# Transposes moved from TensorE to VectorE blocks and DMAs in a one-core hybrid decoder layer

## The chip, the core and the metric

One core of one Trainium2 chip runs the whole layer: TensorE (PE) multiplies matrices, VectorE (DVE) and ScalarE (ACT) work on tiles element by element, GpSimd (POOL) does a few small jobs, and SyncE (SP) issues nearly all of the DMAs. The metric is the device time of one execution in microseconds (us). Lower is better. A time is the median of the runs shown.

## The reference

256 tokens `x` of width 2048 go through one decoder layer in float32: a mixer of mLSTM heads and attention heads, a gated MLP, and a gated addition of a projected side input `p`. Cut to what matters:

```python
h  = rms_norm(x, mix_norm_g)
z  = h @ w_in                                   # 2048 -> 7184 columns
mq, mk, mv, mo, mi, mf, fq, fk, fv, ff = split(z)
ha = mlstm_chunkwise(heads(mq), heads(mk), heads(mv), mi + b, log_sigmoid(mf + b))   # 4 heads of 256
ha = rms_norm(ha, mlstm_out_g) * sigmoid(mo)
qb, kb = rms_norm(fq, fox_q_g), rms_norm(fk, fox_k_g)                                # 8 heads of 128
hb = softmax(qb @ kb.T / sqrt(128) + F[t] - F[s], causal) @ fv    # F: running sum of log_sigmoid(ff + b)
x  = x + concat([ha, hb]) @ w_out                                                   # 2048 -> 2048
a, g = split(rms_norm(x, ffn_norm_g) @ w_up)                                        # 2048 -> 2 x 5632
x  = x + (gelu(causal_dwconv(a)) * g) @ w_down                                      # 5632 -> 2048
x  = x + sigmoid(rms_norm(x, ple_norm_g) @ w_ple_gate) * (p @ w_ple_proj)           # 2048 -> 2048, 256 -> 2048
```

## The kernel before

**Matmuls.** The 256 tokens are two tiles of 128 (NT = 2), the width 2048 is 16 K tiles of 128. Every product is made of three matmuls: weights and activations are each split into a high part `hi` and a remainder `lo`, and hi·hi, hi·lo and lo·hi are summed in PSUM (L291 to L293; L327 to L329 for `quad_group`). The activations stand as the stationary operand, turned (K on the partitions, tokens along the row): `hT`, `catT`, `x2T`, `uT`, `x3T`. So each activation must be transposed between the stage that makes it (tokens on the partitions) and the stage that uses it.

**The stream of weights.** `run_stream` goes through a list of steps. SP loads a block of weights (`raw`, 512 KB, L242), ACT casts it to `hi` (L211), DVE subtracts to get `lo` (L213), PE multiplies. `token_group` makes 8 steps for 512 output columns: a step takes two K tiles and both token tiles, which is 2 x 2 x 3 = 12 matmuls of 128x512. There are 4 raw buffers in the mixing part and 6 in the rest; the split runs 3 (later 4) steps ahead of the matmuls.

**Side work.** Everything else is written as generators in a queue `side`. After each step `pull(2)` advances two of them by one `yield`; a `yield n` puts a generator to sleep for n steps, and `pull(10 ** 6)` runs all to the end. A scheduler then fixes the order of each engine. All DMAs named below are issued by SP in one order, so a load of weights stands behind every small DMA issued ahead of it. Each DMA on SP takes one of eight semaphores in turn and waits for the DMA that had it before.

**Order of the stages.** w_in (attention q, k, v and gates first, then mLSTM q, k, v, o), w_out in four groups of 512 columns (c = 0 to 3), w_up with two passes of w_down, and last the PLE part: for each of four column groups one step of w_ple_proj and eight of w_ple_gate.

**Two ways to transpose stand in the kernel.**

1. On TensorE with an identity matrix (`pe.transpose` into PSUM, then ACT and DVE copy it out): the input (`xT`, L144, in `transpose_x`), the attention weights (`pt`, L657), the gated mLSTM heads (`hap`, L789), `p` (`pTp`, L1118), and column groups 2 and 3 of both residuals (`xT` again, called by `turn_late`), 32 + 24 + 16 + 4 + 32 = 108 transposes of 128x128.
2. On DVE and DMA: `dve.transpose` turns the 32x32 blocks of a tile within their place (L507 for q and k, L843 for the residual), and 16 DMAs of SP carry the blocks to their partitions (`turned`, L870, 32 KB each); L877 (ACT) and L878 (DVE) then scale and split it. The heads' q and k and column groups 0 and 1 of both residuals go this way. `resid(..., nt)` says how many column groups do (`nt` = 2).

Buffers: `mqT0`, `mkT0` and the temporaries `t0` to `t3` have tags of their own; `zb_room` and `sq_rooms` lend the room for the blocks of `turned`.

Of the kernel before, what the change touches and what calls it, by code (L numbers as in the profile page):

```python
# [46 lines left out]
def layer_kernel(  # L47
# [218 lines left out]
    def token_group(w, korder, actT, c0, n, finish, tag="mm", prep=None, load=None, slots=10 ** 6, halved=False):  # L266
# [7 lines left out]
        for bi, (k0, kb) in enumerate(starts):  # L274
            def fn(hi, lo, bi=bi, k0=k0):
                if bi == 0:
                    st["b"] = [(t, 0, n, bank(tag, f"tg{t}")) for t in range(NT)]
                    if halved:
                        st["b"][1:] = [(1, c, c + n // 2, bank(tag, "tg1")) for c in (0, n // 2)]
                final = bi == len(starts) - 1  # L280
                if halved and bi == len(starts) - 2:
                    st["kept"] = [(k0, hi, lo)]
                    return
                for t, c, e, bk in st["b"]:
                    for k, h, l in (st.get("kept", []) if final else []) + [(k0, hi, lo)]:
                        for i in range(h.shape[1]):
                            a = actT()[:, (k + i) % slots, :]
# [3 lines left out]
                            pe.matmul(bk[:, : e - c], ah, h[:, i, c:e], start=first, stop=False)  # L291
                            pe.matmul(bk[:, : e - c], ah, l[:, i, c:e], start=False, stop=False)  # L292
                            pe.matmul(bk[:, : e - c], al, h[:, i, c:e], start=False, stop=last)  # L293
                    if final:
                        finish(t, bk, *((c, e) if halved else ()))
# [74 lines left out]

    dp = ctx.enter_context(tc.tile_pool(name="rows", bufs=1, space=bass.MemoryType.DRAM))
# [10 lines left out]
    with tc.tile_pool(name="mix", bufs=1) as mp:  # L382
        catT = mp.tile([P, KD, 512], F32R, name="catT")
# [99 lines left out]
        def fox_norm(name):  # L483
            def gen():
# [13 lines left out]
                for c in range(2):  # L498
# [3 lines left out]
                    if c == 0:  # L502
                        T = mp.tile([P, 1536], F32, tag="wt", name="fsq")[:, :1024]
                    else:
                        T = mp.tile([P, 4, NT, P], F32, tag="mqT0", name="fsq1").rearrange("p f t r -> p (f t r)")
# [4 lines left out]
                    if name == "fq":  # L510
                        flat = mp.tile([P, 4, NT, P], F32, tag=f"mkT{c}", name="fsy").rearrange("p f t r -> p (f t r)")
                        moved.append((flat, v))
# [17 lines left out]
        g = {}  # L530
# [58 lines left out]
        def row_bcast(tag, h, bufs):  # L589

            v = mp.tile([P, 2, 384], F32, tag=tag, name=tag, bufs=bufs)
            nc.sync.dma_start(out=v.rearrange("p e c -> p (e c)"),
# [3 lines left out]
        def fox_heads():  # L596
            bias, fetched = {}, {}

            def fetch(h0):
                bias[h0] = row_bcast("L", 8 + h0, 3)  # L600
                fetched[h0] = clock[0]

            def first():
                while "em" not in g:
                    yield 1
                for h0 in (0, 2, 4):
# [4 lines left out]
            def gen(pairs):  # L611
                while "em" not in g or len(ready) < 2:
                    yield 1
                zq, zk = zhalves("fq"), zhalves("fk")
# [3 lines left out]
                for h0 in pairs:  # L618
# [35 lines left out]
                    for e in range(2):  # L654
                        pt = bank("aux", "pt")
                        for c in range(3):
                            pe.transpose(pt[:, c * P : (c + 1) * P], L[:, e, c * P : (c + 1) * P], ident)  # L657
                        act.copy(L[:, e], pt[:, 0:384])
                        yield
                    ob = bank("aux", "ob")  # L660
                    for e in range(2):
                        h, o = h0 + e, ob[:, e * 256 : (e + 1) * 256]
                        hs = slice(h * FD, (h + 1) * FD)
                        pe.matmul(o, zv[:, 0, hs], L[:, e, 0:256], start=True, stop=False)  # L664
                        pe.matmul(o[:, 128:256], zv[:, 1, hs], L[:, e, 256:384], start=False, stop=True)
                    for e in range(2):
                        split_T(catT[:, 8 + h0 + e, :], ob[:, e * 256 : (e + 1) * 256])
                    if h0 == 0:
                        fetch(6)
# [7 lines left out]
        def qk_evac(name, grp, done=None):  # L677
            def f(t, b):
                key = name, grp
                if t == 0:  # L680
                    qkT[key] = mp.tile([P, 4, NT, P], F32, name=f"{name}T{grp}")
# [95 lines left out]
        def mlstm_gate(heads):  # L777
            def gen():
                zo, zv = z["mo"], z["mv"]
                for h in heads:  # L780
                    while h not in ha:
                        yield 1
                    bk = bank("aux", "hap")
                    for t in range(NT):
                        hh = zv[:, t, h * 258 : h * 258 + MD]
                        dve.scalar_tensor_tensor(out=hh, in0=hh, scalar=ha[h][:, t : t + 1],
                                                 in1=zo[:, t, h * MD : (h + 1) * MD], op0=ALU.mult, op1=ALU.mult)
                        for i in range(2):
                            pe.transpose(bk[:, i * 256 + t * P : i * 256 + (t + 1) * P],  # L789
                                         hh[:, i * P : (i + 1) * P], ident)  # L790
                    for i in range(2):
                        split_T(catT[:, 2 * h + i, :], bk[:, i * 256 : (i + 1) * 256],
                                scale=g_ml[:, 2 * h + i : 2 * h + i + 1])
# [40 lines left out]
        def resid(c, ssq, dst, gain, room, nt):  # L834
            st = {}

            def f(t, b):
                xc = xs[:, t, c * 512 : (c + 1) * 512]
                dve.tensor_add(xc, b, xc)
                if c < nt:  # L840
                    if t == 0:
                        st["T"], st["Y"] = room()
                    dve.transpose(st["T"][:, :, 4 * t : 4 * t + 4].rearrange("p j f r -> p f j r"),  # L843
                                  xc.rearrange("p (f j r) -> p f j r", f=4, j=4))
# [10 lines left out]
        def turn_late(c, dst, gain):  # L855
            for k0 in (c * 4, c * 4 + 2):
                transpose_x(dst(), k0, gain)
                yield
                yield

        def all_late():
            for job in late:
                yield from job
            late.clear()

        def turned(c, T, Y, dst, gain):

            for n in range(16):
                i, j = divmod(n, 4)
                nc.sync.dma_start(out=Y[32 * j : 32 * j + 32, :, 32 * i : 32 * i + 32], in_=T[32 * i : 32 * i + 32, j])  # L870
                yield
# [15 lines left out]

        kcat = all_k[4:] + all_k[:4]
# [7 lines left out]
        for c in range(4):  # L896
            grp = token_group(w_out, kcat, lambda: catT, c * 512, 512, resid(c, ssq2, get_x2T, g_ffn, zb_room, 2))
            if c == 0:
                grp[4].fn = lambda hi, lo, fn=grp[4].fn: (pull(10 ** 6), fn(hi, lo))
            blocks.extend(grp)  # L900
        run_stream(blocks, 2, ramp=True)
        pull(10 ** 6)
        side.append(all_late())


    with tc.tile_pool(name="ffn", bufs=1) as fp:
# [10 lines left out]
        def tmp(i):  # L917
            return fp.tile([P, 512], F32, tag=f"t{i % 4}", name=f"t{i % 4}")
# [3 lines left out]
        def x2_sums():  # L922
            for i, p in enumerate(S_UP):
                a = tmp(0).rearrange("p (k s) -> p k s", k=2)
                e = tmp(1).rearrange("p (e s) -> p e s", e=4)
# [23 lines left out]
        def up_mid(q):  # L949
            def f(st):  # L950
                t11, t12, t21, t22 = (tmp(i) for i in range(4))
# [23 lines left out]
        def up_evac(q, ag):  # L975
            def f(t, b):
                if ag == 0 and t == 0:
                    sq[q] = fp.tile([P, 2, 4, NT, 4, 32], F32, tag="sq", name="sq")
                z = tmp(2 + t)
# [130 lines left out]
        def load_p():  # L1110
            pr = tmp(3).rearrange("p (t d) -> p t d", t=NT)
            nc.sync.dma_start(out=pr, in_=p[0, 0].rearrange("(t p) d -> p t d", p=P))
            while "bank" not in pT:
                yield 1
            bk = bank("mm", "pTp")
            for k in range(2):
                for t in range(NT):
                    pe.transpose(bk[:, k * 256 + t * P : k * 256 + (t + 1) * P], pr[:, t, k * P : (k + 1) * P], ident)  # L1118
            pT["t"] = x2E.rearrange("p s e c -> p (s e c)")[:, 0:1024].rearrange("p (k c) -> p k c", k=2)
            for k in range(2):  # L1120
                split_T(pT["t"][:, k, :], bk[:, k * 256 : (k + 1) * 256])
            yield

        def down_mid(c, ends):
            def f(st):
                if ends and c == 0:
                    pT["bank"] = True
                xc = [[xs[:, t, (c + n) * 512 : (c + n + 1) * 512] for n in range(2)] for t in range(NT)]
                a, b = tmp(0), tmp(1)
# [11 lines left out]
        def down_end(c, ends):  # L1141
            room = sq_rooms()
            done = [resid(c + n, ssq3, get_x3T, g_ple, lambda n=n: room(n), 2) for n in range(2)] if ends else None
# [34 lines left out]
        def proj_done(t, b):  # L1178
            pj[t] = b

        def gate_done(c0, n):
            sg = {}

            def f(t, b, i=0, j=n):
                if "r" not in r3:
                    r3["r"] = rstd_of(ssq3, "ple")
                if i == 0:
                    sg[t] = tmp(c0 // 256 + t)
                w = (j - i) // (2 if i else 1)
                for c in range(i, j, w):  # L1190
                    sc = sg[t][:, c : c + w]
                    act.activation(sc, b[:, c - i : c - i + w], AF.Sigmoid, scale=r3["r"][:, t : t + 1])
                    dve.tensor_mul(sc, sc, pj[t][:, c : c + w])
# [5 lines left out]
        for c0 in range(0, D, 512):  # L1199
            if c0 == 0:  # L1200
                blocks[-1].fn = lambda hi, lo, fn=blocks[-1].fn: (fn(hi, lo), side.append(all_late()))
            blocks.extend(token_group(w_ple_proj, [0], lambda: pT["t"], c0, 512, proj_done, tag="aux"))
            blocks.extend(token_group(w_ple_gate, all_k, get_x3T, c0, 512, gate_done(c0, 512),
                                      halved=c0 == D - 512))
# [31 lines left out]
```

## Time and profile before

| | |
|---|---|
| median of 3 runs | 1248.66 us (1248.21 to 1248.93) |
| the profiled execution | 1247.05 us, of which the span of instructions is 1245.3 us |
| granted TensorE clock | 0.999 of full speed |
| busy: PE, DVE, ACT, POOL | 1239.0 (99%), 895.0 (72%), 682.2 (55%), 92.1 us (7%) |
| DMA moved | 258.79 MB; mean 208 GB/s |

The busy time of an engine is the sum of its instructions; the chain of waits is followed back from the last instruction and names what set the end. A row of the groups of instructions reads: line, engine, operation, output <- input, shape, count, then the busy time of the group, the mean time of one in ns, and the idle time ahead of them with what ended it. A row of the timeline reads: start, duration (both us), engine, line, operation, count. Matmuls are pipelined, so their durations overlap, and the distance from start to start is what one costs. A row of the DMA issues reads: transfer, queue, count, KB each, median us from the issue to the landing.

### The profile page before, as it was taken

What the parts mean: (1) busy time and instruction counts of PE and PEld (TensorE: products, weight loads), DVE (VectorE), ACT (ScalarE), POOL (GpSimd) and SP (SyncE); (2) the same over time, 40 slices, a digit from 0 to 9 for tenths busy, and PEclk for the clock granted to TensorE, in tenths of its full rate; (3) what the DMA queues carried; (4) which work ended last, traced back from release to release, by engine and by line L of the source; (5) the groups of instructions that cost most, each with busy time, mean ns of one, the idle gap of its engine ahead of it and who ended that gap; (6) DMA issues with size and microseconds to landing.
All of it is one profiled execution on the core that took longest, in us unless ns stands there. A gap on an engine that the chain in (4) does not pass through costs nothing.

```text
span 1245.3 us, 16201 instructions
## 1 busy us (share of the span) xinstructions
PE 1239.0 (99%) x5669; PEld 1042.4 (84%) x5669; DVE 895.0 (72%) x1153; ACT 682.2 (55%) x955; POOL 92.1 (7%) x134
## 2 busy tenths in 40 slices
PE   9999999999999999999999999999999999999998
PEld 7899988888888888888888888888888888888887
DVE  6455566555565666787988797968888889978554
ACT  8555445446554455564566555455566546556542
POOL 2000000000000000121022010002012112000000
PEclk9999999999999999999999999999999999999999
DMA  8667877864557766676686665676577666777661
GB/s 289 174 180 224 252 239 209 211 186 133 165 177 200 229 226 198 210 237 200 195 276 224 190 223 195 203 223 204 172 264 237 200 225 202 223 204 250 206 208 50
DMA packets 161858, 258.79 MB, mean 208 GB/s; under 512 B 38377, under 2 KB 65905, under 8 KB 161777
## 3 DMA queue, kind: packets, MB, share of 16 engines
q1 hardware_dynamic: 161168, 257.57, 66.4%
q8 instruction: 44, 0.72, 0.2%
q14 instruction: 37, 0.30, 0.1%
q10 hardware_dynamic: 385, 0.16, 0.0%
q0 software_dynamic: 224, 0.03, 0.0%
HBM read 237.76 MB, written 2.12 MB: 193 GB/s over the span
## 4 chain that ended last, share of the span: by engine, by line
PE 99%; DMA 0%; SPq 0%; DVE 0%; ACT 0%; issue 0%; DVEq 0%
PE qgD L327 16%; PE qgD L328 16%; PE qgD L329 16%; PE tg L291 14%; PE tg L293 14%; PE tg L292 14%; PE qgQ L328 2%; PE qgQ L327 2%; PE qgQ L329 2%; PE xT L144 1%; PE mob L755 0%; DMA xs<-in_x_dram 0%; PE sc L636 0%; PE ob L664 0%; PE msc L730 0%; PE pt L657 0%
## 5 line engine op out<-in xcount | busy, mean ns | idle before, releaser
L213 DVE TENSOR_TENSOR lo<-raw,hi 128x1024 fp32r<-128x1024 f32 (+3 forms) x495 | 585.2, 1193 | 284.5 <-ACT hi L211 277.3
L211 ACT CAST hi<-raw 128x1024 fp32r<-128x1024 f32 (+3 forms) x495 | 497.4, 1017 | 434.1 <-PE qgD L329 182.4
L328 PE MATMUL qgD<-lo,x2T 128*128 128x512 f32 x580 | 225.7, 389 | 0.0
L329 PE MATMUL qgD<-hi,x2T 128*128 128x512 f32 x580 | 225.6, 389 | 0.0
L327 PE MATMUL qgD<-hi,x2T 128*128 128x512 f32 x580 | 219.8, 389 | 0.0
L291 PE MATMUL tg<-hi,hT 128*128 128x512 f32 (+2 forms) x480 | 182.0, 383 | 0.0
L292 PE MATMUL tg<-lo,hT 128*128 128x512 f32 (+2 forms) x480 | 180.3, 378 | 0.0
L293 PE MATMUL tg<-hi,hT 128*128 128x512 f32 (+2 forms) x480 | 180.2, 379 | 0.0
L328 PEld LDWEIGHTS qgD<-lo,x2T 128*128 128x128 f32 x580 | 108.9, 188 | 22.7 <-DVE lo L213 0.3
L329 PEld LDWEIGHTS qgD<-hi,x2T 128*128 128x128 f32 x580 | 108.9, 188 | 22.6
L327 PEld LDWEIGHTS qgD<-hi,x2T 128*128 128x128 f32 x580 | 108.9, 188 | 22.6
L329 PE MATMUL qgD<-hi,uT 128*128 128x512 f32 x296 | 115.2, 389 | 0.0
L328 PE MATMUL qgD<-lo,uT 128*128 128x512 f32 x296 | 115.2, 389 | 0.0
L327 PE MATMUL qgD<-hi,uT 128*128 128x512 f32 x296 | 105.9, 390 | 0.0
L293 PEld LDWEIGHTS tg<-hi,hT 128*128 128x128 f32 x480 | 89.9, 188 | 12.7
L292 PEld LDWEIGHTS tg<-lo,hT 128*128 128x128 f32 x480 | 90.2, 188 | 12.2
L291 PEld LDWEIGHTS tg<-hi,hT 128*128 128x128 f32 x480 | 90.0, 188 | 12.0
L327 PEld LDWEIGHTS qgD<-hi,uT 128*128 128x128 f32 x296 | 55.3, 188 | 12.0 <-ACT hi L211 0.7
L328 PEld LDWEIGHTS qgD<-lo,uT 128*128 128x128 f32 x296 | 55.6, 188 | 11.7 <-DVE lo L213 0.2
L329 PEld LDWEIGHTS qgD<-hi,uT 128*128 128x128 f32 x296 | 55.6, 188 | 11.5
L1028 POOL TENSOR_TENSOR Y<-sq,Y 128x256 f32<-128x256 f32 x44 | 50.6, 1180 | 54.5 <-ACT sq L1024 54.5
L291 PE MATMUL tg<-hi,x3T 128*128 128x512 f32 (+1 forms) x144 | 52.7, 367 | 0.0
(271 smaller groups left out, 1410.1 us busy)
## 6 DMA issues: line engine op xcount, KB each, us to landing
raw<-in_w_up_dram SPq DMA_DIRECT2D x176, 512.0 KB, 5.1
raw<-in_w_down_dram SPq DMA_DIRECT2D x88, 512.0 KB, 4.7
raw<-in_w_in_dram SPq DMA_DIRECT2D x79, 512.0 KB, 4.2
raw<-in_w_out_dram SPq DMA_DIRECT2D x32, 512.0 KB, 3.9
raw<-in_w_ple_gate_dram SPq DMA_DIRECT2D x32, 512.0 KB, 4.7
Y<-sq SPq DMA_DIRECT2D x176, 64.0 KB, 2.0
raw<-in_w_in_dram SPq DMA_DIRECT2D x24, 416.0 KB, 3.6
raw<-in_w_in_dram SPq DMA_DIRECT2D x16, 408.0 KB, 3.8
```

The lines of the kernel that those rows point to most:

```text
L144: pe.transpose(bk[:, t * P : (t + 1) * P], xs[:, t, k * P : (k + 1) * P], ident)
L211: act.copy(hi[:, :w], raw[:, :w])
L213: dve.tensor_sub(lo[:, :w], raw[:, :w], f32(hi[:, :w]))
L291: pe.matmul(bk[:, : e - c], ah, h[:, i, c:e], start=first, stop=False)
L292: pe.matmul(bk[:, : e - c], ah, l[:, i, c:e], start=False, stop=False)
L293: pe.matmul(bk[:, : e - c], al, h[:, i, c:e], start=False, stop=last)
L327: pe.matmul(st[bk], ah, hi[:, cols], start=first, stop=False)
L328: pe.matmul(st[bk], ah, lo[:, cols], start=False, stop=False)
L329: pe.matmul(st[bk], al, hi[:, cols], start=False, stop=final)
L1028: pool.tensor_tensor(out=u[:, f], in0=c[:, :, :, f].rearrange("p i t r -> p t i r"), in1=g[:, :, :, f].rearrange("p i t r -> p t i r"), op ...
```

## The change

Only the 32 transposes of the input stay on TensorE. The other 76 are replaced by DVE's 32x32 transposes with 16 DMAs for each tile:

- attention weights: a 128x768 tile (two heads) is turned by one `dve.transpose` into a room `early`, and 16 DMAs of 32x192 carry the blocks back into `L`; the product with V (`ob`) then reads `L` through a view in pieces of 32 columns. Both pairs of a generator go through softmax and DMAs first, and the products come at least 3 steps after the last DMA;
- gated mLSTM heads: two heads go into a 128x1024 tile `hag`, one `dve.transpose` (`hsq`), 16 DMAs (`hsy`), then scaling and splitting into `catT`; `catT` is cut in two halves, the first of which shares its room with `early`;
- `p`: the same with a 128x512 tile (`pr`);
- residuals: `resid(..., nt)` gets nt = 3 for w_out and 4 for the last w_down pass. All column groups are turned by `turned`; groups from `nt` on wait in `late` (here w_out's c = 3, pulled at the start of the FFN).

In `turned`, the DMAs of PLE's groups and of the late groups come four at a wake of the generator. The order of K tiles changes in three places: w_out's c = 0 and c = 1 are interleaved (6 + 6 + 2 + 2 steps), w_up's q = 0 has its two groups interleaved (6 + 6 + 2 + 2), and in PLE the last four gate steps of column group 0 come after the projection and the first four gate steps of column group 512. Temporaries share two 128x1024 tiles, `spare(0)` and `spare(1)`.

The diff, cut to its core:

```diff
-                    for e in range(2):
-                        pt = bank("aux", "pt")
-                        for c in range(3):
-                            pe.transpose(pt[:, c * P : (c + 1) * P], L[:, e, c * P : (c + 1) * P], ident)
-                        act.copy(L[:, e], pt[:, 0:384])
-                        yield
+                    flat = L.rearrange("p e c -> p (e c)")
+                    dve.transpose(T.rearrange("p j g r -> p g j r"), flat.rearrange("p (g j r) -> p g j r", g=6, j=4))
+                    yield
+                    for i in range(4):
+                        for j in range(4):
+                            nc.sync.dma_start(out=flat[32 * j : 32 * j + 32, 192 * i : 192 * i + 192],
+                                              in_=T[32 * i : 32 * i + 32, j].rearrange("p g r -> p (g r)"))
+                        yield 1
+                    sent[h0] = clock[0]
+                for h0 in pairs:
+                    if clock[0] < sent[h0] + 3:
+                        yield sent[h0] + 3 - clock[0]
...
-                        pe.matmul(o, zv[:, 0, hs], L[:, e, 0:256], start=True, stop=False)
-                        pe.matmul(o[:, 128:256], zv[:, 1, hs], L[:, e, 256:384], start=False, stop=True)
+                        pe.matmul(o, zv[:, 0, hs], W[:, e, 0:2], start=True, stop=False)
+                        pe.matmul(o[:, 128:256], zv[:, 1, hs], W[:, e, 2], start=False, stop=True)
...
-                if c < nt:
-                    if t == 0:
-                        st["T"], st["Y"] = room()
-                    dve.transpose(st["T"][:, :, 4 * t : 4 * t + 4].rearrange("p j f r -> p f j r"),
-                                  xc.rearrange("p (f j r) -> p f j r", f=4, j=4))
+                if t == 0:
+                    st["T"], st["Y"] = room()
+                dve.transpose(st["T"][:, :, 4 * t : 4 * t + 4].rearrange("p j f r -> p f j r"),
+                              xc.rearrange("p (f j r) -> p f j r", f=4, j=4))
                 if t == NT - 1:
-                    if c < nt:
-                        side.append(turned(c, st["T"], st["Y"], dst, gain))
-                    else:
-                        late.append(turn_late(c, dst, gain))
+                    (side if c < nt else late).append(turned(c, st["T"], st["Y"], dst, gain, dst is not get_x2T))
...
-        def turned(c, T, Y, dst, gain):
+        def turned(c, T, Y, dst, gain, ffn):
+            if c == 1 and not ffn:
+                yield 2
             for n in range(16):
                 i, j = divmod(n, 4)
                 nc.sync.dma_start(out=Y[32 * j : 32 * j + 32, :, 32 * i : 32 * i + 32], in_=T[32 * i : 32 * i + 32, j])
-                yield
+                if ffn and c < 2:
+                    yield
+                elif j == 3:
+                    yield 1
             yield 3
...
+            if c == 1:
+                blocks[-2:] = grp[:6] + blocks[-2:] + grp[6:]
...
-                for ag in range(2):
-                    blocks.extend(token_group(w_up, all_k, lambda: x2, ag * FF, 512, up_evac(q, ag),
-                                              tag=("aux", "mm")[ag]))
+                g0, g1 = (token_group(w_up, all_k, lambda: x2, ag * FF, 512, up_evac(q, ag), tag=("aux", "mm")[ag])
+                          for ag in range(2))
+                blocks.extend(g0[:6] + g1[:6] + g0[6:] + g1[6:])
...
+            if c0 == 512:
+                blocks[-4:] = grp[:5] + blocks[-4:] + grp[5:]
```

What this does to the order of the engines is seen at two places. The first is the start of PLE, which follows the last pass of w_down. SP before, from the raw block of the eighth gate step on (`raw273` is the projection's second block):

```order
L242 DMA raw272_9868<-in_w_ple_gate_dram 128x2x512
L242 DMA raw273_9886<-in_w_ple_proj_dram 128x2x512
L242 DMA raw274_9926<-in_w_ple_gate_dram 128x2x512
L242 DMA raw275_9956<-in_w_ple_gate_dram 128x2x512
L242 DMA raw276_9986<-in_w_ple_gate_dram 128x2x512
L242 DMA raw277_10014<-in_w_ple_gate_dram 128x2x512
L242 DMA raw278_10032<-in_w_ple_gate_dram 128x2x512
```

and now (`turnT` to `turnY` are the residual's blocks of groups 2 and 3, one tile for both):

```order
L242 DMA raw272_9925<-in_w_ple_gate_dram 128x2x512
L242 DMA raw273_9943<-in_w_ple_gate_dram 128x2x512
L892 DMA turnY_9950<-turnT_9949 32x8x32 x8
L242 DMA raw274_9987<-in_w_ple_gate_dram 128x2x512
L892 DMA turnY_9950<-turnT_9949 32x8x32 x8
L242 DMA raw275_10015<-in_w_ple_gate_dram 128x2x512
L892 DMA turnY_9950<-turnT_9949 32x8x32 x8
L242 DMA raw276_10043<-in_w_ple_gate_dram 128x2x512
L892 DMA turnY_9950<-turnT_9949 32x8x32 x8
L242 DMA raw277_10069<-in_w_ple_gate_dram 128x2x512
```

32 small DMAs stand between ten blocks that are loaded ahead and the later ones, eight ahead of each block. Steps 0 to 9 of PLE use `raw264` to `raw273` and K tiles 0 to 7; step 10 uses `raw274` and K tiles 8 and 9. ACT at the same place, before:

```order
L135 ACTIVATE x3T_9697<-xT8_9912,vT_104 128x256
L135 ACTIVATE x3T_9697<-xT9_9917,vT_104 128x256
L135 ACTIVATE x3T_9697<-xT10_9942,vT_104 128x256
L135 ACTIVATE x3T_9697<-xT11_9947,vT_104 128x256
L211 CAST hi_10028<-raw272_9868 128x1024
L211 CAST hi_10046<-raw273_9886 128x1024
L135 ACTIVATE x3T_9697<-xT12_9972,vT_104 128x256
L135 ACTIVATE x3T_9697<-xT13_9977,vT_104 128x256
```

and now:

```order
L211 CAST hi_10101<-raw273_9943 128x1024
L211 CAST hi_10121<-raw274_9987 128x1024
L211 CAST hi_10149<-raw275_10015 128x1024
L211 CAST hi_10175<-raw276_10043 128x1024
L902 ACTIVATE x3T_9755<-turnY_9950,vT_104 128x256 x8
L211 CAST hi_10193<-raw277_10069 128x1024
```

The eight casts that fill K tiles 8 to 15 of `x3T` now stand behind the cast of `raw276`, in one piece. The second place is the end of w_out and the start of w_up. SP before (`turn` holds the blocks of group 1):

```order
L870 DMA turn_3518<-turn_3518 32x8x32 x3
L242 DMA raw148_3627<-in_w_out_dram 128x2x512
L242 DMA raw149_3647<-in_w_out_dram 128x2x512
L242 DMA raw150_3667<-in_w_out_dram 128x2x512
L242 DMA raw151_3687<-in_w_out_dram 128x2x512
L242 DMA raw152_3713<-in_w_out_dram 128x2x512
L242 DMA raw0_3863<-in_w_up_dram 128x2x512
L242 DMA raw1_3865<-in_w_up_dram 128x2x512
```

and now (`turn_3755` holds the blocks of group 2, whose matmuls end eight steps ahead of the first w_up step):

```order
L242 DMA raw150_3728<-in_w_out_dram 128x2x512
L242 DMA raw151_3746<-in_w_out_dram 128x2x512
L892 DMA turn_3755<-turn_3755 32x8x32 x4
L242 DMA raw152_3777<-in_w_out_dram 128x2x512
L892 DMA turn_3755<-turn_3755 32x8x32 x12
L242 DMA raw0_3951<-in_w_up_dram 128x2x512
L242 DMA raw1_3953<-in_w_up_dram 128x2x512
```

The first block of w_up is now issued behind twelve small DMAs. Over the whole program PE loses 76 matmuls (the transposes) and 8 ACT copies go with them; SP has 1026 DMAs in place of 850 (64 more for the attention weights, 32 for the mLSTM heads, 16 for `p`, 64 for the residuals), and DVE has 15 more block transposes (4 of 128x768, 2 of 128x1024, 9 of 128x512).

More of the change, by code (lines that the diff above doesn't have):

```diff
@@ L369, in quad_group, with spare @@
         return steps
+    def spare(i, name):
+        return bp.tile([P, 1024], F32, tag=f"spare{i}", name=name)
     dp = ctx.enter_context(tc.tile_pool(name="rows", bufs=1, space=bass.MemoryType.DRAM))
@@ L382, in layer_kernel, with cat @@
     with tc.tile_pool(name="mix", bufs=1) as mp:
-        catT = mp.tile([P, KD, 512], F32R, name="catT")
+        early = mp.tile([P, 3, 768], F32, tag="cat0", name="early")
+        cats = {1: mp.tile([P, 8, 512], F32R, name="cat1")}
+        def cat(k):
+            if k < 8 and 0 not in cats:
+                cats[0] = mp.tile([P, 8, 512], F32R, tag="cat0", name="cat0")
+            return cats[k // 8][:, k % 8]
         tri = mp.tile([P, P], F32, name="tri")
@@ L779, in gen @@
                 zo, zv = z["mo"], z["mv"]
[L780 to L783, printed above, removed]
+                while heads[1] not in ha or len(WT) < MH or len(sent) < 5:
+                    yield 1
+                h4, T, Y = mp.tile([P, 1024], F32, tag="mkT1", name="hag"), spare(0, "hsq"), spare(1, "hsy")
+                for n, h in enumerate(heads):
                     for t in range(NT):
-                        hh = zv[:, t, h * 258 : h * 258 + MD]
-                        dve.scalar_tensor_tensor(out=hh, in0=hh, scalar=ha[h][:, t : t + 1],
+                        dve.scalar_tensor_tensor(out=h4[:, 512 * n + 256 * t : 512 * n + 256 * t + MD],
+                                                 in0=zv[:, t, h * 258 : h * 258 + MD], scalar=ha[h][:, t : t + 1],
@@ new lines, in gen @@
+                T4 = T.rearrange("p (j g r) -> p j g r", j=4, g=8)
+                dve.transpose(T4.rearrange("p j g r -> p g j r"), h4.rearrange("p (g j r) -> p g j r", g=8, j=4))
+                yield
+                for i in range(4):
+                    for j in range(4):
+                        nc.sync.dma_start(out=Y[32 * j : 32 * j + 32, 256 * i : 256 * i + 256],
+                                          in_=T4[32 * i : 32 * i + 32, j].rearrange("p g r -> p (g r)"))
+                    yield 1
@@ new lines, in gen @@
+                yield 3
+                V = Y.rearrange("p (b h t i r) -> p h i t b r", b=4, h=2, t=NT, i=2)
+                for n, h in enumerate(heads):
+                    for i in range(2):
+                        hi, lo = (cat(2 * h + i)[:, e * 256 : (e + 1) * 256].rearrange("p (t b r) -> p t b r", t=NT, b=4)
+                                  for e in range(2))
+                        gain = g_ml[:, 2 * h + i : 2 * h + i + 1]
+                        act.activation(hi, V[:, n, i], AF.Copy, scale=gain)
+                        for t in range(NT):
+                            dve.scalar_tensor_tensor(out=lo[:, t], in0=V[:, n, i, t], scalar=gain, in1=f32(hi[:, t]),
+                                                     op0=ALU.mult, op1=ALU.subtract)
@@ L950, in f @@
             def f(st):
-                t11, t12, t21, t22 = (tmp(i) for i in range(4))
+                (t11, t12), (t21, t22) = temps(0), temps(1)
                 act.copy(t22, st["Q1"])
@@ L1142, in down_end @@
             room = sq_rooms()
-            done = [resid(c + n, ssq3, get_x3T, g_ple, lambda n=n: room(n), 2) for n in range(2)] if ends else None
+            done = [resid(c + n, ssq3, get_x3T, g_ple, lambda n=n: room(n), 4) for n in range(2)] if ends else None
             def f(t, n, b):
```

127 lines of the change are left out of this document (68 added, 59 removed).

## Prediction

> **What bounds the kernel now.** I read the busy table first, then the chain of waits, then the waits by engine. From the page:
>
> ```profile
> PE 1239.0 (99%) x5669; PEld 1042.4 (84%) x5669; DVE 895.0 (72%) x1153; ACT 682.2 (55%) x955; POOL 92.1 (7%) x134
> ...
> PE 99%; DMA 0%; SPq 0%; DVE 0%; ACT 0%; issue 0%; DVEq 0%
> ```
>
> The first line has TensorE busy for 1239.0 of the span's 1245.3 us, the second says that the chain that ends last is TensorE for 99%. A busy PE could still be a slow one, so the waits follow, TensorE's own first:
>
> ```profile
> PE warm L84 <- DVE ones L80: 1.1, 1, 1.1
> PE xT L144 <- DMA xs<-in_x_dram: 1.0, 1, 1.0
> ```
>
> ```profile
> ACT hi L211 <- PE qgD L329: 182.4, 134, 3.0
> ACT hi L211 <- PE tg L293: 169.0, 117, 2.4
> ```
>
> TensorE waits twice, both times at the start, 2.1 us in all. ACT, the first link of the supply of weights, waits 351 us for TensorE to free buffers. So the supply runs ahead of TensorE, and what is taken out of TensorE's own sequence comes off the end, as long as nothing becomes late by it.
>
> **What the 76 transposes cost.** Their groups:
>
> ```profile
> L657 PE MATMUL pt<-ident,L 128*128 128x128 f32 x24 | 3.6, 272 | 0.0
> ...
> L789 PE MATMUL hap<-ident,zb 128*128 128x128 f32 x16 | 2.4, 272 | 0.0
> ```
>
> 272 ns is a pipelined duration, so I take the distance between starts. One group of three `pt` and one of four `xT` in the timeline:
>
> ```profile
> 220.29 0.40 PE L293 MATMUL tg<-hi,hT 128*128 128x512 f32 x1
> 220.53 0.49 PE L657 MATMUL pt<-ident,L 128*128 128x128 f32 x3
> 220.78 0.49 PE L291 MATMUL tg<-hi,hT 128*128 128x512 f32 x1
> 221.10 0.39 PE L292 MATMUL tg<-lo,hT 128*128 128x512 f32 x1
> ```
>
> ```profile
> 435.49 0.39 PE L291 MATMUL tg<-hi,x2T 128*128 128x512 f32 x1
> 435.71 0.39 PE L292 MATMUL tg<-lo,x2T 128*128 128x512 f32 x1
> 435.94 0.39 PE L293 MATMUL tg<-hi,x2T 128*128 128x512 f32 x1
> 436.17 0.60 PE L144 MATMUL xT<-ident,xs 128*128 128x128 f32 x4
> 436.53 0.48 PE L291 MATMUL tg<-hi,x2T 128*128 128x512 f32 x1
> 436.84 0.40 PE L292 MATMUL tg<-lo,x2T 128*128 128x512 f32 x1
> 437.08 0.40 PE L293 MATMUL tg<-hi,x2T 128*128 128x512 f32 x1
> ```
>
> Undisturbed, one matmul follows another after 0.227 us (435.49 to 436.17 in three). With four transposes the second matmul behind them starts 0.67 us after the group, in place of 0.227: 0.445 us lost. With three it is 221.10 - 220.53 - 0.227 = 0.345. There are 24 `pt` in eight threes and 52 others (16 `hap`, 32 late `xT`, 4 `pTp`) in thirteen fours: 8 x 0.345 + 13 x 0.445 = 8.5 us. Behind a group the distance stays at 0.24 for a while (436.84 to 437.08); if that lasts ten matmuls at 0.005 to 0.01, it is 0.05 to 0.1 us for each of 21 groups, 1 to 2 us at most. I take 9.0 us, with ends of 8.4 and 10.
>
> The Trainium skill speaks against the change: "VectorE: DVE Perf Modes", section Rules for kernel authors, says to transpose 128x128 on TensorE if PSUM may be the destination, and its section on the three transpose paths gives 390 ns there and 311 ns on VectorE for 32x32 blocks only (in bf16). By 390 ns of TensorE time each, an estimate from that page, the saving would be 30 us; by this trace's starts it is 0.11 us each, and the trace decides.
>
> **What takes their place.** Durations of the operations that are added, and the transfers:
>
> ```profile
> L507 DVE STREAM_TRANSPOSE fsq<-zb 128x1024 f32<-128x1024 f32 x4 | 4.7, 1220 | 0.0
> ...
> L877 ACT ACTIVATE x3T<-turnY,vT 128x256 fp32r<-128x256 f32 x8 | 3.4, 504 | 2.3 <-DMA turnY<-turnT 2.3
> ...
> L878 DVE SCALAR_TENSOR_TENSOR x3T<-turnY,vT,x3T 128x256 fp32r<-128x256 f32 x8 | 3.3, 481 | 1.6 <-ACT x3T L877 1.6
> ...
> L843 DVE STREAM_TRANSPOSE turnT<-xs 128x512 f32<-128x512 f32 x4 | 2.7, 690 | 0.0
> ```
>
> ```profile
> raw<-in_w_ple_gate_dram SPq DMA_DIRECT2D x32, 512.0 KB, 4.7
> ...
> xs<-in_x_dram SPq DMA_DIRECT2D x8, 256.0 KB, 7.2
> ...
> turnY<-turnT SPq DMA_DIRECT2D x32, 32.0 KB, 3.8
> ```
>
> DVE: 9 x 0.69 + 2 x 1.22 + 4 x about 0.95 (128x768, between the two) = 12.5 us over the span, on an engine at 72% that is not in the chain. ACT gives up eight copies. The casts and subtractions of `catT`, `x2T` and `x3T` stay as many, from SBUF instead of PSUM, 0.50 and 0.48 us. The reading of `L` in pieces of 32 columns by `ob` I cost at nothing: the chain has two matmuls of `sc`, which already reads such pieces, and two of `ob`, which reads whole rows, at the same 0.43:
>
> ```profile
> 208.64 0.43 PE sc L636 x2
> ...
> 226.92 0.43 PE ob L664 x2
> ```
>
> What can cost time is SP: 176 more DMAs in one queue, ahead of loads. Its price and what it may delay:
>
> ```profile
> 1084.86 5.84 SPq L870 DMA_DIRECT2D turnY<-turnT  x9
> ```
>
> ```profile
> 527.39 10.87 SPq L993 DMA_DIRECT2D Y<-sq  x16
> 538.36 3.94 SPq L242 DMA_DIRECT2D raw<-in_w_up_dram  x6
> ```
>
> One small DMA holds the queue for 0.65 us (5.84 / 9); a load takes some 0.5. The second fence shows sixteen in a piece that hold six loads back by 10.9 us, and TensorE has no wait there: the loads run that far ahead. I go through the new places by this measure.
>
> *Attention weights.* Eight bursts of four DMAs can meet in about five steps: 26 x 0.65 = 17 us of queue and five loads, in 13.6 us of matmuls. The loads lag by 5 to 6 us against the 10.9 just seen. The order keeps three steps (8.2 us) from the last DMA to the product, against 3.8 us of landing. Nothing waits. What is behind: `early`'s room is `catT`'s first half, written by the mLSTM heads long after.
>
> *mLSTM heads and p.* 16 DMAs per pair of heads, 10.4 us, plus 3.8 of landing and four casts: about 18 us after `hag`. The heads' K tiles are moved to w_out's last steps of groups 0 and 1 (6 + 6 + 2 + 2), and the flush of side jobs two steps later, which gives that time. `p` is loaded during the last w_down pass, with tens of us to spare. Nothing.
>
> *w_out to w_up.* Before, the first w_up matmul and its load:
>
> ```profile
> 433.45 0.39 PE L291 MATMUL tg<-hi,x2T 128*128 128x512 f32 x1
> ```
>
> ```profile
> 420.99 13.68 SPq L242 DMA_DIRECT2D raw<-in_w_up_dram  x9
> ```
>
> The load goes out 12.5 us ahead of its use. Now twelve DMAs of group 2 (7.8 us) stand in front of it. Group 2's matmuls end 8 x 2.72 = 21.8 us ahead of that use (a step is 12 x 0.227); two additions and two block transposes later (some 3 us) 16 DMAs begin, so `raw0` goes out about 8.5 us ahead, lands after 3.9 to 5 (3.5 to 4.6 ahead), and cast and subtraction (2.3 us) leave 1.2 to 2.3 us. Zero, with a thin cover: gone, it costs up to 2 us.
>
> *w_down to PLE, the place that decides.* Call E the end of w_down's matmuls. DVE's rows there:
>
> ```profile
> 1139.04 0.68 DVE L839 TENSOR_TENSOR xs<-qgD,xs 128x512 f32<-128x512 f32 x1
> 1139.64 1.21 DVE L213 TENSOR_TENSOR lo<-raw,hi 128x1024 fp32r<-128x1024 f32 x1
> 1140.77 1.87 DVE L839 TENSOR_TENSOR xs<-qgD,xs 128x512 f32<-128x512 f32 x3
> 1142.57 1.21 DVE L213 TENSOR_TENSOR lo<-raw,hi 128x1024 fp32r<-128x1024 f32 x1
> ```
>
> PLE began at E = 1140.3, and the additions end at E + 2.3. With two block transposes between them group 2's second one ends at about E + 3.6. Then SP issues 28 DMAs up to group 2's last, with three loads between: E + 3.6 + 28 x 0.65 + 3 x 0.5 = E + 23.3. It lands 3.8 later, E + 27.1; the first cast gives K tile 8's high part at E + 27.6, its low part 0.5 later. TensorE asks for K tile 8 after ten steps, E + 27.2. So a stall of about 0.5 us; 0 if the DMAs land in 3 us, 1.8 if they take as long as the loads' 4.7 and the low part binds. Next late: K tile 12 (last DMA issued at about E + 26, ready near E + 31 against E + 32.6) and `raw277`, whose cast stands behind the eight casts (E + 33 against E + 35.4). Both hold.
>
> The sum: -9.0 + 0 (DVE, ACT, `ob`) + 0 (w_up) + 0.5 (PLE) = -8.5 us. On the profiled execution of 1247.05 that is 1238.6; the median of the runs is 1.6 us above it, so 1248.66 - 8.5 = 1240.2.
>
> **The rivals.**
>
> - *A longer stall at PLE*, 1.5 to 6 us: for it speaks that the 32 DMAs need 20.8 us of a queue that must also bring a load each 2.72 us, and that the landing of 3.8 was measured with fewer of them in a row. It gives 1241 to 1246.
> - *A stall at w_up* because `raw0` is late: a thin 1.2 us of cover; 1 to 3 us, 1241 to 1243.
> - *Slower, by the eight DMAs in turn.* Every DMA on SP waits for the eighth before it. While a landing takes under 8 x 0.65 = 5.2 us, the pitch is 0.65; above it the pitch is landing / 8. If landings here took T, K tile 8 would be ready at E + 3.6 + 31 x T/8 + T + 1. At T = 6.4 that is E + 35.8 and the whole saving is gone; slower by over 0.2% from T = 6.9 on; with the 7.2 of the input's loads, E + 39.7, a stall of 12.5 and 1252. For it: 32 KB in 128-byte pieces, in the part with the densest loads. Against it: the same transfers took 3.8 at 1085, between loads as well. The Trainium skill has this rule too: "DMA: Bandwidth & Descriptors", section Rules for kernel authors, holds that many small transfers should be coalesced because under 64 KB mostly overhead is paid. The trace agrees on the overhead (3.8 us for 32 KB), and not that it must be on the path.
> - *The change doesn't do what it says:* TensorE takes the time back as waits on `lo`, because the supply can't go faster. Against it stand the 351 us of ACT waiting for TensorE; DVE would go from 72% to about 74%. It would give 1245 to 1249.
>
> **How the numbers follow.** Within 0.2%, 2.5 us, no difference from before can be told: 1246.2 to 1251.2. The forecast (saving 8.4 to 10, stall under 1.5; 1238.5 to 1241.5): 0.57. The longer PLE stall: 0.18. The w_up stall: 0.09. DMAs in turn: 0.07, of which 0.03 ends within 0.2% and 0.04 above. The supply: 0.05, most of it within 0.2%. Some 0.04 are left for a saving above 10. Faster is 0.57 + 0.18 + 0.09 + 0.04 and a little of the others, 0.88; same 0.07; slower 0.05. The range takes in the forecast and most of the first two rivals: 1238.2 to 1245.
>
> **What would show it.** TensorE's busy time should fall by 8 to 10 us. Its waits should hold the two rows of the start, and one new of about 0.5 us on `x3T` K tile 8 (released by ACT L902 or DVE L903). A wait on `lo` (L213) at the first w_up step would be the second rival; a row of `turnY` that lands in over 5 us, with SP's pitch above 0.65, the third; many small waits on `lo` all along the span, the last. I am wrong if TensorE's waits grow by more than 5 us in all, or if its busy time falls by less than 7.

## The result and the profile after

The changed kernel takes 1240.95 us (median of 6 runs, 1239.79 to 1242.63) against 1247.99 (6 runs, 1247.28 to 1248.93). The ratio is 0.9944, 95% interval 0.9931 to 0.9956: 7.0 us faster. Forecast were 8.5 us and 1240.2. The profiled execution took 1241.52, with a span of 1239.8 against 1245.3 before, 5.5 us less: the execution of before that was profiled is 0.9 us under its median, that of the changed kernel 0.6 above.

The engines' busy time and the chain that ended last, from the page of the changed kernel:

```profile
PE 1231.6 (99%) x5593; PEld 1035.4 (84%) x5593; DVE 905.0 (73%) x1176; ACT 679.2 (55%) x947; POOL 91.3 (7%) x134
...
PE 94%; DMA 3%; DVE 1%; SPq 1%; ACT 1%; issue 0%; DVEq 0%; ACTq 0%
```

76 instructions are gone from TensorE, and 7.4 us of its busy time. The chain, 99% TensorE before, now goes through other engines for 6% of the span. What TensorE waits for (engine, line, what it waited for, us in total, times, longest):

```profile
PE qgD L328 <- ACT hi L211: 1.4, 1, 1.4
PE warm L84 <- DVE ones L80: 1.1, 1, 1.1
PE xT L144 <- DMA xs<-in_x_dram: 0.9, 1, 0.9
PE tg L293 <- DVE lo L213: 0.5, 1, 0.5
```

The first and the last are new. The last is at the first w_up matmuls, in the timeline (start, duration, what, idle before):

```profile
429.33 0.73 PE L292 MATMUL tg<-hi,x2T 128*128 128x512 f32 x2
430.59 0.50 PE L293 MATMUL tg<-lo,x2T 128*128 128x512 f32 x1 [0.53 <-DVE lo L213]
```

The other lies in the last w_down pass, 29 us ahead of PLE:

```profile
1107.80 0.39 PE L330 MATMUL qgD<-hi,uT 128*128 128x512 f32 x1
1109.64 1.19 PE L328 MATMUL qgD<-hi,uT 128*128 128x512 f32 x4 [1.45 <-ACT hi L211]
1110.90 0.50 PE L329 MATMUL qgD<-lo,uT 128*128 128x512 f32 x1
```

There 1109.64 - 1107.80 = 1.84 stand in place of 0.23. To compare kernels I add up all distances from start to start of TensorE's instructions that exceed 0.43 us, from 9 us on, less 0.23 each ("stalls" below). Before has none. The changed kernel has 2.5 us (0.7 at w_up, 1.6 + 0.2 in w_down), and none at the start of PLE, where the forecast had its stall. So, by these two profiles, 5.5 us of span are 8.0 saved and 2.5 given back.

### The profile page after: what moved, and what is told of

Read it like the earlier page. It is cut to its first block, busy times and chain, and to the rows that moved or that the text cites. A ratio compares the mean times of both kernels' runs of the same rounds, so it can differ in the third digit from the quotient of the medians.

```text
span 1239.8 us, 16294 instructions
## 1 busy us (share of the span) xinstructions
PE 1231.6 (99%) x5593; PEld 1035.4 (84%) x5593; DVE 905.0 (73%) x1176; ACT 679.2 (55%) x947; POOL 91.3 (7%) x134
## 4 chain that ended last, share of the span: by engine, by line
PE 94%; DMA 3%; DVE 1%; SPq 1%; ACT 1%; issue 0%; DVEq 0%; ACTq 0%
PE qgD L329 16%; PE qgD L330 16%; PE qgD L328 16%; PE tg L292 14%; PE tg L293 14%; PE tg L294 14%; PE qgQ L330 1%; PE qgQ L329 1%; PE qgQ L328 1%; DMA raw<-in_w_out_dram 1%; DVE lo L213 1%; SPq L892 1%; DMA turnY<-turnT 1%; ACT hi L211 1%; DMA raw<-in_w_down_dram 0%; PE mob L776 0%
## 5 line engine op out<-in xcount | busy, mean ns | idle before, releaser
L213 DVE TENSOR_TENSOR lo<-raw,hi 128x1024 fp32r<-128x1024 f32 (+3 forms) x495 | 584.7, 1192 | 258.3 <-ACT hi L211 237.4
L293 PE MATMUL tg<-lo,x3T 128*128 128x512 f32 (+1 forms) x144 | 52.7, 366 | 0.0
```

Source lines behind the costliest of these rows:

```text
L213: dve.tensor_sub(lo[:, :w], raw[:, :w], f32(hi[:, :w]))
```

## The experiments

| run | us, median | ratio to before (95%) | span of the profile | stalls in it |
|---|---|---|---|---|
| changed kernel, again | 1242.80 | 0.9954 (0.9941 to 0.9966) | 1241.5 | 2.9 |
| e1_pool | 1243.22 | 0.9962 (0.9949 to 0.9976) | 1241.5 | 3.8 |
| e2_late | 1244.16 | 0.9971 (0.9960 to 0.9983) | 1240.6 | 3.8 |
| e3_both | 1244.69 | 0.9972 (0.9961 to 0.9984) | 1243.6 | 6.2 |
| e4_dummy | 1249.16 | 1.0002 (0.9993 to 1.0011) | 1247.9 | 0.9 |
| e5_pleorder | 1251.49 | 1.0017 (1.0004 to 1.0030) | 1249.1 | 10.3 |
| e6_more | 1249.83 | 1.0011 (1.0000 to 1.0022) | 1245.8 | 8.2 |
| changed kernel, third time | 1241.09 | 0.9950 (0.9937 to 0.9962) | 1239.4 | 2.5 |
| e7_stagger | 1240.71 | 0.9936 (0.9922 to 0.9949) | 1239.1 | 1.8 |
| e8_all | 1241.11 | 0.9944 (0.9931 to 0.9957) | 1240.7 | 2.2 |

The first four were timed side by side, then the next three, then the last three, each time with the kernel before.

**Are the stalls there each time?** The changed kernel was run twice more.

> The changed kernel once more, as the yardstick of the three that follow. Theory: 7 us under the kernel before (ratio 0.9944), with two stalls of TensorE in its profile, 0.7 us at the first w_up matmul (lo of the first block late) and 1.6 + 0.2 us in the last w_down pass (hi late). Rival (the two stalls were chance of one execution): they are gone from this profile, and the time is then near 1238.5.

> The changed kernel again, beside the next two: 7 us under the kernel before at the first timing, 5.7 at the second, so 5.5 to 7.5, and the same two places of waiting in the profile (w_up's first matmul 0.7 us, last w_down pass 1.6 to 1.9).

The gains were 4.9 and 6.1 us in the medians, the first less than the 7 expected. Both profiles have the same two places (the last matmul ahead of the wait starts at 431.07 and 429.29 for the first, at 1109.89 and 1107.57 for the second), with the same 0.7 and 1.3 to 1.4 us. They belong to the kernel and not to one execution.

**What a transpose costs.** e4_dummy puts 76 transposes back that nobody reads, in groups of four:

```diff
             if i >= 0:
                 steps[i].fn(*parts.pop(i))
+                if ramp and 10 <= i < 67 and i % 3 == 1:
+                    bk = bank("aux", "dm")
+                    for n in range(4):
+                        pe.transpose(bk[:, n * P : (n + 1) * P], xs[:, 0, n * P : (n + 1) * P], ident)
```

> 76 transposes whose result nobody reads are put back onto TensorE: 19 groups of four 128x128 transposes of the input, one behind every third step of w_in from the 11th on, while the rest is the changed kernel. Theory: a transpose in TensorE's sequence costs 0.11 us and a little in the matmuls behind it: 19 x 0.445 = 8.5, up to 9.4 us slower than the changed kernel, as slow as or slower than the kernel before. Rival: the transposes were worth less than the starts show, since the stream of weights gives part of it back; then 5 to 7 us slower.

Without its stalls this profile lasts 1247.0 us. The three profiles of the changed kernel last 1237.2, 1238.6 and 1236.9 without theirs, 1237.6 in the mean: the transposes add 9.4, at the top of what was expected. In the measured time only 6 to 7 us arrive (ratio 1.0002 against 0.9944 to 0.9954), and the kernel is as slow as the one before. Of the difference, 1.6 to 2 us are stalls that are gone: the w_up stall is not there and the one in w_down is half. Both statements hold, the theory's for TensorE's sequence and the rival's for the time. Why the stalls shrink is not shown. The last of these transposes runs at 178 us, and at w_up the same twelve DMAs stand ahead of the first load; it goes out 6.6 us ahead of its first matmul (at 432.99, the matmul at 439.61), in place of 5.0.

**What bounds K tile 8 at the start of PLE.** e6_more issues the first four DMAs of groups 2 and 3 twice (8 more):

```diff
+                if ffn and c >= 2 and i == 0:
+                    nc.sync.dma_start(out=Y[32 * j : 32 * j + 32, :, 32 * i : 32 * i + 32], in_=T[32 * i : 32 * i + 32, j])
```

> Eight more small DMAs at the start of PLE: the first four of the 16 of column groups 2 and 3 are issued twice, into the same place. Theory: SP's 0.65 us for each is on the path there and the changed kernel has next to no cover left (0.1 us of waiting on K tile 8 in its profile), so TensorE waits 8 x 0.65 = 5.2 us more on K tile 8: 4.5 to 5.5 us slower than the changed kernel. Rival: the DMAs overlap with waits that SP has anyway, and under 2 us come through.

TensorE at that place:

```profile
1162.61 0.39 PE L294 MATMUL tg<-hi,x3T 128*128 128x512 f32 x1
1168.03 0.80 PE L292 MATMUL tg<-hi,x3T 128*128 128x512 f32 x1 [5.03 <-ACT x3T L904]
```

A wait of 1168.03 - 1162.61 - 0.23 = 5.2 us: 8 x 0.65 to the tenth. SP's time per DMA is on the path there, and the changed kernel has next to no cover left (K tile 8's first cast ends at 26.8 us after w_down there and at 32.3 here). By the medians it is 7.0 to 8.7 us, more than the 4.5 to 5.5 expected. The two kernels were not timed side by side, and the kernel before took 0.5 to 1.4 us more beside this one; but another part is in the trace. Behind the wait the matmuls are slower:

```profile
1168.62 0.63 PE L293 MATMUL tg<-lo,x3T 128*128 128x512 f32 x1
1169.05 0.63 PE L292 MATMUL tg<-hi,x3T 128*128 128x512 f32 x1
1169.47 0.63 PE L293 MATMUL tg<-lo,x3T 128*128 128x512 f32 x1
```

They start 0.43 us apart in place of 0.23, up to 1172.0. The granted clock of TensorE is 0.72 in the mean from 1168 to 1175, and 1.00 in the changed kernel over the same stretch. From 1168.03 to 1172.24, ten distances take 4.2 us in place of 2.3: 1.9 more, of which the column of stalls counts 0.4. So the wait cost 5.2 + 1.9 = 7.1 us of TensorE's time, which fits the medians; the execution that was profiled is the fastest of its nine, with a span 5.6 us above the mean of the changed kernel's three. The profile of e5_pleorder shows the same behind its waits at PLE (0.72 in the mean from 1162 to 1168); that of e3_both does not behind a single wait of 2.7 us (1.00). How long a wait must be for this was not tested.

e5_pleorder takes the old order of PLE's steps, with a flush of the side jobs ahead of the step that uses K tile 8:

```diff
-            if c0 == 512:
-                blocks[-4:] = grp[:5] + blocks[-4:] + grp[5:]
-            else:
-                blocks.extend(grp)
+            if c0 == 0:
+                grp[5].fn = lambda hi, lo, fn=grp[5].fn: (pull(10 ** 6), fn(hi, lo))
+            blocks.extend(grp)
```

> PLE's steps in the old order (projection and eight gate steps of column group 0, then group 512), all transposes as in the changed kernel; the side jobs are run to the end ahead of the step that uses K tile 8. Theory: K tiles 8 and 9 are asked for 13.6 us after the end of w_down and are there after 26 to 27, so TensorE waits 12 to 13 us: about 1253, slower than the kernel before. Rival: the 32 DMAs are ready much sooner when asked for, and the new order buys little: a stall under 5 us.

Slower than the kernel before, but by less than expected: 7.0 us of stalls at PLE. The edit did not undo the order. The scheduler itself moved the projection and two gate steps of group 512 ahead of the steps that use K tile 8, so TensorE had two to three steps more to do than the edit had meant, and its waits there are spread over `hi`, `lo` and `x3T`. Neither number of the expectation is confirmed. By the ratios this kernel is 8 to 9 us slower than the changed one; how much of that is the order of the steps and how much the flush that came with it is not separated.

**Why w_down stalls.** ACT in the changed kernel, and then in the kernel before, at the same place of the program:

```profile
1100.89 1.05 ACT L211 CAST hi<-raw 128x1024 fp32r<-128x1024 f32 x1 [0.40 <-DVE raw L361]
1105.34 3.31 ACT L902 ACTIVATE x3T<-turnY,vT 128x256 fp32r<-128x256 f32 x8 [3.39 <-DMA turnY<-turnT]
1108.56 4.40 ACT L211 CAST hi<-raw 128x1024 fp32r<-128x1024 f32 x5
```

```profile
1110.54 0.92 ACT L877 ACTIVATE x3T<-turnY,vT 128x256 fp32r<-128x256 f32 x2 [2.27 <-DMA turnY<-turnT]
1111.36 1.04 ACT L211 CAST hi<-raw 128x1024 fp32r<-128x1024 f32 x1
1112.30 2.51 ACT L877 ACTIVATE x3T<-turnY,vT 128x256 fp32r<-128x256 f32 x6
```

Each engine runs its instructions in the order that the scheduler fixed. Before, the late cast of weights stood behind two casts of `x3T`; now it stands behind all eight, waits 3.4 us with them for the turning DMAs and then 3.3 us for the casts, and TensorE waits for it. The diff does not touch the code of this place, and why the scheduler came to another order stays open. That the order makes the stall is tested by three runs, e1_pool, e3_both (below) and e7_stagger. e1_pool gives the eight casts to GpSimd:

```diff
-                act.activation(hi, src, AF.Copy, scale=gain[:, k : k + 1])
+                if ffn and c < 2:
+                    pool.tensor_scalar_mul(hi, src, gain[:, k : k + 1])
+                else:
+                    act.activation(hi, src, AF.Copy, scale=gain[:, k : k + 1])
```

> The eight casts that fill K tiles 0 to 7 of x3T are made by GpSimd in place of ACT; all else as in the changed kernel. Theory: the stall of 1.8 us in the last w_down pass comes from ACT's order, in which these eight casts stand ahead of the hi of a weight block that has already landed, and wait there for the turning DMAs. Then the stall is gone, and the time falls by 1.5 to 1.8 us against the changed kernel (ratio to the kernel before about 0.993); a remainder of 0.3 is possible, since VectorE still has one subtraction of x3T ahead of that block's lo. Rival: the block itself lands late, behind the small DMAs in SP's queue; then the stall stays, and the time with it.

The wait at this place falls from 1.6 + 0.2 to 0.2 us, as the theory says, but the time does not fall: 1.6 us of waits on `hi` come up at 1118.9, 8 us later, and 1.0 at PLE. The row of GpSimd and that of VectorE's part there:

```profile
L903 POOL TENSOR_SCALAR x3T<-turnY,vT 128x256 fp32r<-128x256 f32 x8 | 11.5, 1454 | 66.8 <-DMA turnY<-turnT 66.8
```

```profile
L906 DVE SCALAR_TENSOR_TENSOR x3T<-turnY,vT,x3T 128x256 fp32r<-128x256 f32 x8 | 5.3, 658 | 3.7 <-DMA raw<-in_w_down_dram 3.3 <-POOL x3T L903 0.4
```

A cast takes 1.45 us in the mean on GpSimd against 0.50 on ACT, and VectorE, whose subtractions wait for them one by one, gets to its additions of weights (L361) later; ACT then waited 7.5 us for these. The wait had gone over to the next engine. e7_stagger leaves the engines and spaces the groups out:

```diff
+            if ffn and c % 2 == 1:
+                yield 6 if c == 1 else 4
```

> Group 1 of the last residual starts its DMAs six steps after group 0, and group 3 four steps after group 2; nothing else is touched. In ACT's order the four casts of group 1 then stand behind the hi cast that was late, and at the start of PLE the four of group 2 stand right behind the hi of the block before they are asked for. Theory (ACT's fixed order makes the w_down stall, SP's queue bounds K tile 8): the 1.6 to 1.9 us in w_down are gone, K tile 8 is ready at about E + 20 in place of E + 26.5, K tile 12 at about E + 31 against E + 32.6, and the time is 1.5 to 2 us under the changed kernel. Rival (the supply in w_down is short whatever the order, as when GpSimd made the casts): the stall turns up again a few us later, and less than 0.7 us is gained.

Four casts now stand on either side of the late one:

```profile
1096.54 1.71 ACT L904 ACTIVATE x3T<-turnY,vT 128x256 fp32r<-128x256 f32 x4 [0.51 <-DMA turnY<-turnT]
...
1103.86 2.00 ACT L211 CAST hi<-raw 128x1024 fp32r<-128x1024 f32 x2 [0.40 <-DVE raw L361]
1105.86 1.71 ACT L904 ACTIVATE x3T<-turnY,vT 128x256 fp32r<-128x256 f32 x4
```

TensorE's waits:

```profile
PE xT L144 <- DMA xs<-in_x_dram: 1.5, 1, 1.5
PE warm L84 <- DVE ones L80: 1.1, 1, 1.1
PE tg L293 <- DVE lo L213: 0.5, 1, 0.5
PE qgD L328 <- ACT hi L211: 0.2, 1, 0.2
```

The 1.2 to 1.4 us on `hi` are 0.2. K tile 8's cast ends 20.0 us after the end of w_down, against 26.5 to 26.9 in the changed kernel and the 20 that were expected. Some 0.9 us of new small stalls lie at 1045 to 1053, so 0.7 us less in all; the start of this execution was slower by a microsecond (1.5 us on the input's load). The ratio is 0.9936 against 0.9950 of the changed kernel beside it, 1.7 us, with intervals that overlap; the medians differ by 0.4. The mechanism is shown by the waits, the size of the gain is not settled. It has the lowest median and ratio of all that were run, but not clear of the noise.

**Why w_up stalls.** SP in the changed kernel ahead of w_up's first matmul at 429.3, and in e2_late, which turns group 2 only after w_up has begun:

```profile
411.98 2.82 SPq L892 DMA_DIRECT2D turn<-turn  x4
414.90 0.54 SPq L242 DMA_DIRECT2D raw<-in_w_out_dram  x1
415.49 8.74 SPq L892 DMA_DIRECT2D turn<-turn  x12
424.32 11.91 SPq L242 DMA_DIRECT2D raw<-in_w_up_dram  x10
```

```profile
416.38 14.08 SPq L242 DMA_DIRECT2D raw<-in_w_up_dram  x9
431.48 2.55 SPq L896 DMA_DIRECT2D turn<-turn  x4
```

```diff
-                              resid(c, ssq2, get_x2T, g_ffn, zb_room if c < 3 else spare_room, 3))
+                              resid(c, ssq2, get_x2T, g_ffn, (zb_room, zb_room, None, spare_room)[c], 3))
...
+        side.append(turn_c2())      # the two block transposes, then turned(2, ...)
         side.append(x2_sums())
...
-                blocks.extend(g0[:6] + g1[:6] + g0[6:] + g1[6:])
+                blocks.extend(g0[:4] + g1[:4] + g0[4:6] + g1[4:6] + g0[6:] + g1[6:])
```

> Column group 2 of the first residual is turned at the start of w_up in place of during w_out's last group, so that no small DMA stands ahead of w_up's first blocks; w_up's first stage uses K tiles 0 to 7 of both its groups first (4 + 4 + 2 + 2 + 2 + 2 steps), so that tiles 8 to 11 are asked for 21.8 us after the start. Theory: the first blocks go out some 8 us earlier, the 0.7 us stall at the first w_up matmul is gone, and no new one comes: 0.7 us under the changed kernel, with the w_down stall left. Rival: 32 small DMAs among w_up's first blocks hold these back, and a stall of 1 us or more comes up at steps 8 to 14 of w_up.

> Both edits, GpSimd's casts in w_down and the later turning of group 2. Theory: the two stalls are independent and all that was lost of the saving, so the time is 2.2 to 2.5 us under the changed kernel, near 1238.5 (ratio to the kernel before about 0.9925), and TensorE waits only at the start. Rival: the stalls are symptoms of one supply that is short, and with the one gone the other grows: 1 us or less is gained.

> The staggered groups and, besides, group 2 of the first residual turned at the start of w_up, as in the run with that edit alone. Theory: the first w_up stall is gone too (0.7 us), but the last DMAs of the first residual's group 3 come some 30 us after w_up's start and K tile 12, asked for at 32.6, stalls by 0.3 to 1.8 us, as it did in the two runs with that edit; so it is even with or up to 1 us slower than the staggered one. Rival: without the turn of the side jobs that these runs had, K tile 12 is in time and 0.7 us more are gained.

The load goes out 8 us earlier, and the stall at the first matmul is gone in all three: the twelve DMAs had used its cover up (e4_dummy kept them and, with 1.6 us more of cover, had no stall either). But the time did not fall. K tile 12 of `x2T` stalled at W + 32 by 0.35, 1.8 and 0.9 us, W being w_up's first matmul, as its last DMAs are now issued some 30 us after W. In e2_late and e3_both K tile 8 of `x3T` stalled as well, by 1.5 and 2.7 us, though nothing was edited there: ACT made the four casts of group 3 ahead of those of group 2, most likely because one more job in the queue had shifted the turn in which `pull` takes its jobs. e8_all, with the staggered groups, has no stall there, which fits that; it came out as expected, with 0.9 us at K tile 12 and 0.4 us slower than e7_stagger in the medians. e3_both's expectation of independent stalls fell with this.

## Why the prediction was right

Direction, time and range were right: 1240.95 lies 0.75 us above the forecast time. That it came so near is in part luck. The kernel before took 0.7 us less here than the figure that the forecast started from; the gain was 7.0 us here against the sum of 8.5, and 4.9 and 6.1 in the two later timings. By the profiles the terms are -8.0 + 0.7 (w_up) + 1.8 (w_down) + 0 (PLE) = -5.5: one term was put at zero and is not, and one is missing from the sum.

- *The bound.* TensorE's own sequence set the end, and what was taken out of it came off. Confirmed by removing 76 transposes (8.0 us without stalls) and by adding 76 (9.4). TensorE's busy time fell by 7.4 us, less than the 8 to 10 named as the sign, and its waits grew by 1.8, from 2.1 to 3.9.
- *The saving*, 9.0 with ends of 8.4 and 10. Removal gave 8.0 in one profile (7.7 by the mean of three), adding gave 9.4; the profiles of one kernel differ by 1.7 us, so the term holds within that and no closer. The Trainium skill's "VectorE: DVE Perf Modes", section Rules for kernel authors (TensorE for 128x128 if PSUM will do), did not hold where TensorE is the bound: by this pair of kernels 7 us of 1248 lie on the other side.
- *DVE, ACT, `ob`, attention, mLSTM, p at nothing.* No wait of TensorE lies in those stages. In the sum for the attention weights, eight bursts of four are 32 DMAs and not 26; by the same sum the loads would lag by 9.7 us in place of 5 to 6, still under the 10.9 that it compares with.
- *The start of PLE*, 0.5 us, was nearly right as a time, and right in that SP's queue sets it: K tile 8's first cast ended at E + 26.8 in place of the E + 27.6 of the sum (E = 1136.65, SP's first DMA at E + 3.0, group 2's last at E + 23.5), with no stall to speak of. That last DMA had landed by the cast's start at E + 26.3, in 2.8 us or less and not 3.8. What ACT waited for last was another transfer of the same queue, the load ahead of it in ACT's order:

```profile
1161.99 1.05 ACT L211 CAST hi<-raw 128x1024 fp32r<-128x1024 f32 x1 [4.85 <-DMA raw<-in_w_ple_gate_dram]
1162.94 3.54 ACT L902 ACTIVATE x3T<-turnY,vT 128x256 fp32r<-128x256 f32 x8
```

  So the casts of `x3T` stood behind a late cast of weights here, the reverse of w_down; the sum had the small DMA's landing in its place. e6_more then showed that eight further DMAs are paid in full.
- *w_up, zero with 1.2 us of cover.* The rival came true: 0.7 us. The load went out 5.0 us ahead and not 8.5. The burst began at W - 17.4 and not at W - 18.8 (W is w_up's first matmul, 429.3), and took 12.3 us up to the load and not 10.4: a load of w_out stands in it, and its twelve DMAs took 8.74 us (the row above) in place of 7.8, as one of them held the queue for 1.6 us.
- *The step that failed:* the prediction went through the places that the diff names and took the order elsewhere as given. In w_down the order of ACT changed without an edit, and it cost 1.8 us, more than all the costs that the sum had (0.5). The order of the changed program, which stood to be read ahead of any run, has the eight casts in one row there; I read it at PLE and w_up only.
- *The rivals.* DMAs in turn: the landings of `turnY` did not come near 6.4 us in the median, they got shorter (3.8 before):

```profile
turnY<-turnT SPq DMA_DIRECT2D x64, 32.0 KB, 3.2
```

  The supply: TensorE did not take the time back in many small waits, but in two places at single instructions, and e1 to e3 show that these move when one is taken away.

## What to carry to other kernels

Where TensorE is 99% busy and waits for nothing, each transpose in its sequence costs its start-to-start time (0.11 us here), and VectorE with small DMAs can take them; the price is paid in the DMA queue, 0.65 us each here, ahead of whatever load stands behind. When such a kernel is changed, read the fixed order of every engine at all places where it differs, not at the edited ones alone: a cast that waits for a late DMA ahead of a cast that is ready cost more than any step that was edited. And try to take a stall away by spacing the work out on the engine that has it: here that took the wait away, with a gain in time too small to tell from the noise, while giving the work to a slower engine moved the wait to the next. A wait can cost more than its length: behind 5.2 us the matmuls ran at half pace for some 4 us more.

## What was not expected of the hardware

While GpSimd made its casts, VectorE's subtractions from SBUF took 0.66 us in the mean (the row above) against 0.48 with ACT's casts; the last of the eight, when GpSimd was at its end, took 0.48 again. The order of the two engines does not explain a longer instruction, so they seem to get in each other's way. GpSimd's casts point the same way: they took from 0.92 us, with VectorE idle or mostly in one of these subtractions, to 1.77 and 2.29 beside VectorE's subtractions of weights (L213), which themselves kept their 1.21. It was not tested by itself.
